# Two-layer hybrid trunk on one core: the next queries' projection issued ahead of the sliding keys' transposes, and the second layer's mixer norm at raised priority

## The chip, the core and the metric

The kernel runs on one core of one Trainium2 chip. The metric is the device time of one execution, in microseconds (us), as the median of repeated runs. In the code and in the profile the engines are PE (TensorE, the matmuls), DVE (VectorE), ACT (ScalarE), POOL (GpSimd) and SP (SyncE, which here issues the DMA transfers).

## What is computed

The reference is a trunk of two residual layers over 256 tokens of width 2048, all in float32. Layer 0 has the "even" mixer, layer 1 the "odd" one; behind each come a gated feed-forward part with a short convolution and a gated embedding. Cut to what matters here:

```python
for i in range(2):
    h = rms_norm(x, attn_norm[i])
    if i == 0:                                   # even mixer
        proj = h @ w_in_even[0]
        c_q, c_kv, k_idx, w_idx, qb, kb, vb = split(proj)
        # A: indexer scores pick the top 64 keys, then attention with
        #    q = rms_norm(rms_norm(c_q) @ w_uq) over the latents c_kv
        y_a = dsa_attention(c_q, c_kv, k_idx, w_idx, ...)
        # B: sliding-window attention, keys kb normed per head
        y_b = swa_sink_attention(qb, kb, vb, ...)
        y = concat(y_a, y_b) @ w_out_even[0]
    else:                                        # odd mixer
        y = forgetting_attention(h @ w_in_odd[0], ...) @ w_out_odd[0]
    x = x + y
    x = x + conv_ffn(rms_norm(x, ffn_norm[i]), ...)
    gate = sigmoid(rms_norm(x, ple_norm[i]) @ w_ple_gate[i])
    x = x + gate * (p[i] @ w_ple_proj[i])
```

## The kernel before

**Products.** The 256 tokens are two blocks `b` of 128 rows; the residual `x` stays on the chip in four column chunks `xs[b][j]` of 512. Every large product is made of matmuls of 128 by 128 by 512. `load` (L104) brings a piece of a weight of 1 MB into `raw`, which has three buffers; `granule` splits each half of it into a rounded high part `whi` on ACT (L116) and the rest `wlo` on DVE (L117), five buffers each. `Acc.add` (L144) then issues three matmuls for each pair of tiles (high by high, high by low, low by high) into two PSUM banks `ps_mm`, one for each block; three banks go round under that tag. A piece of 1 MB feeds 24 matmuls, and its `raw` buffer is free for the next load when DVE has made the second `wlo`.

**Norm.** `norm` (L177 to L195) makes the transposed, split left operand of a projection. For each chunk `j` and block `b` it multiplies `xs[b][j]` by a gain that SP loads (L177, two buffers), on DVE into a tile `xg` (L190), transposes that on PE in four pieces (L171, PSUM tag `ps_ax`, two banks), and splits the result with ACT (L123) and DVE (L124) into tiles called `n` (mixer norms) or `np` (gate norm). The row scale `rstd` is put on later, behind the product.

**Even mixer.** `proj_a(c)` makes the queries of four A heads: two products with `w_uq` (`cc`), each copied out of PSUM by ACT into an `xg` tile (L469), squared (L472) and transposed on PE (L211) into `qaT`, which DVE copies (L216); then comes a reciprocal square root, a chain of small DVE steps (L75 to L84). After `proj_a(0)` the indexer's scores and the top-64 search (L503, L504) run on DVE. Then the keys and values of the B heads are projected; each block's keys go into a tile `kk` of tag `xg` (L524), are squared and summed (`ssq_heads`), scaled by the reciprocal square root of the sums (`heads_rstd`, L328 to L331; L531) and transposed into `kbT` (L211, L214). `proj_a(1)` follows, then the values `vA` of the A heads (L547), the first A attention `att_a(0)` and the B queries (`proj_b`).

**Buffers and order.** The pool `work` has tags `xg`, `y` and `junk` with two buffers each. A framework orders the instructions: each engine's row is fixed before the run by a scheduler that takes instructions in the order of the code, unless a block stands in `tc.high_priority(offset=PR)`, with PR = 300, which lets its instructions go ahead of work that stands before it in the code. The gate norm in `ple_gate` (`np`) stands in such a block; the odd mixer's norm (`n1`) does not. An engine works through its row in order, so an instruction that waits holds all that stands behind it. SP's row holds all loads.

Of the kernel before, what the change touches and what calls it, by code (L numbers as in the profile page):

```python
# [9 lines left out]
F32 = mybir.dt.float32  # L10
# [6 lines left out]
P = 128  # L17
# [21 lines left out]
PR = 300  # L39
# [9 lines left out]
def trunk(ctx, tc, t, onehot, out):  # L49
# [7 lines left out]
    work = ctx.enter_context(tc.tile_pool(name="work", bufs=2))  # L57
# [12 lines left out]
    def rsqrt(dst, src, n, scale, post=1.0):  # L70

        v, y, a = (sm.tile([P, NT, 8], F32, tag="rq_" + c, name="rq_" + c)[:, :, :n] for c in "vya")
        if len(src.shape) == 2:
            v, y, a = v[:, :, 0], y[:, :, 0], a[:, :, 0]
        nc.vector.tensor_scalar(v, src, scale, EPS, op0=ALU.mult, op1=ALU.add)  # L75
        nc.vector.tensor_scalar(a.bitcast(I32), v.bitcast(I32), 1, None, op0=ALU.logical_shift_right)
        nc.vector.tensor_scalar(y.bitcast(I32), a.bitcast(I32), -1.0, MAGIC, op0=ALU.mult, op1=ALU.add)
        for it in range(3):
            nc.vector.scalar_tensor_tensor(a, y, -0.5, v, op0=ALU.mult, op1=ALU.mult)
            nc.vector.tensor_tensor(a, a, y, op=ALU.mult)  # L80
            last = it == 2
            nc.vector.scalar_tensor_tensor(dst if last and post == 1.0 else y, a, 1.5, y, op0=ALU.add, op1=ALU.mult)
        if post != 1.0:
            nc.vector.tensor_scalar(dst, y, post, None, op0=ALU.mult)  # L84
# [64 lines left out]
    def moving(src, c0, ncols, lhs, nktiles, nk=4):  # L149
        a = Acc(ncols, nktiles)  # L150
        a.add(src, c0, lhs, list(range(nktiles)), nk)
        return a.ps
# [5 lines left out]
    def make_ht(name):  # L158

        h = HT()  # L160
        h.t = [gp.tile([P, 4, 2, S], F32R, tag=f"ht{j}", name=f"{name}{j}") for j in range(4)]
        h.lhs = lambda k, b: tuple(h.t[k // 4][:, k % 4, m, b * P:(b + 1) * P] for m in range(2))
        h.rhs = lambda k: tuple(h.t[k // 4][:, k % 4, m, :] for m in range(2))
        h.both = lambda k: h.t[k // 4][:, k % 4].rearrange("p m s -> p (m s)")
        return h

    def transpose_split(h, j, b, src, tag="ax"):

        pt = psum(tag)
        for i in range(4):  # L170
            nc.tensor.transpose(pt[:, i * P:(i + 1) * P], src[:, i * P:(i + 1) * P], ident)  # L171
        split_evict(h.t[j][:, :, 0, b * P:(b + 1) * P], h.t[j][:, :, 1, b * P:(b + 1) * P],
                    pt.rearrange("p (a c) -> p a c", a=4))

    def load_gain(gain, j):
        g = gp.tile([P, 512], F32, tag="gbc", name="gain", bufs=2)
        nc.sync.dma_start(g, bcast_rows(gain[j * 512:(j + 1) * 512], 512))  # L177
        return g

    def norm(gain, name, loaded=()):  # L180

        h = make_ht(name)
        rstd = sm.tile([P, NT], F32, tag="rstd", name="rstd")
        h.rstd = [rstd[:, b:b + 1] for b in range(NT)]
        accs = sm.tile([P, NT, 4], F32, tag="ssx", name="ssx")
        for j in range(4):
            g = loaded[j] if j < len(loaded) else load_gain(gain, j)
            for b in range(NT):
                xg = work.tile([P, 512], F32, tag="xg", name="xg")
                nc.vector.tensor_tensor(xg, xs[b][j], g, op=ALU.mult)  # L190
                transpose_split(h, j, b, xg)
                junk = work.tile([P, 512], F32, tag="junk", name="junk")
                nc.scalar.activation(junk, xs[b][j], AF.Square, accum_out=accs[:, b, j:j + 1])
        tot = sm.tile([P, NT], F32, tag="sst", name="sst")
        nc.vector.tensor_reduce(tot, accs, axis=AX.X, op=ALU.add)  # L195
        rsqrt(rstd, tot, 1, 1.0 / D)
        return h
# [9 lines left out]
    def transpose_to(dst, src, n, parts=P, scale=None, eng="v"):  # L207

        pt = psum()
        for i in range(n):  # L210
            nc.tensor.transpose(pt[:, i * parts:(i + 1) * parts], src[:, i * P:(i + 1) * P], ident[:parts, :parts])  # L211
        v = pt[:, :n * parts].rearrange("p (a c) -> p a c", a=n)
        if scale is not None:
            nc.scalar.activation(dst, v, AF.Copy, scale=scale)  # L214
        elif eng == "v":
            nc.vector.tensor_copy(dst, v)  # L216
        else:
            nc.scalar.copy(dst, v)
# [97 lines left out]
    def ssq_heads(pool, ps, nh, dst):  # L316

        sq = work.tile([P, 512], F32, tag="junk", name="junk")
        nc.scalar.activation(sq[:, :nh * HD], ps, AF.Square)
        nc.vector.tensor_reduce(dst, sq[:, :nh * HD].rearrange("p (h d) -> p h d", h=nh), axis=AX.X, op=ALU.add)  # L320

    def heads_rstd(ssq, n, rx, width, post=1.0):


        r = sm.tile([P, NT, 8], F32, tag="hr", name="hr", bufs=HR)[:, :, :n]
        tmp = sm.tile([P, NT, 8], F32, tag="hrt", name="hrt")[:, :, :n]
        for b in range(NT):
            nc.vector.tensor_scalar(tmp[:, b], ssq[:, b], rx[b], rx[b], op0=ALU.mult, op1=ALU.mult)  # L328
        rsqrt(r, tmp, n, 1.0 / width)
        for b in range(NT):  # L330
            nc.vector.tensor_scalar(r[:, b], r[:, b], rx[b], post, op0=ALU.mult, op1=ALU.mult)  # L331
        return r


    def even_mixer(i, e):
        W = t["w_in_even"][e]
        with ExitStack() as es:
# [22 lines left out]
            h = norm(t["attn_norm"][i], "n0", gains)  # L360
# [98 lines left out]
            def proj_a(c):  # L459
                qT = []  # L460
                rqs = sm.tile([P, NT, 4], F32, tag="rqa", name="rqa", bufs=4)
                sqs = sm.tile([P, NT, 4], F32, tag="sqa", name="sqa")
                for cc in range(2):
                    ps = moving(t["a_w_uq"][e], (c * 2 + cc) * 512, 512, cq_lhs, 4)
                    qTc = ev.tile([P, 4, S], F32, tag="qT", name="qaT", bufs=6)
                    qT.append(qTc)
                    for b in range(NT):
                        qr = work.tile([P, 512], F32, tag="xg", name="xg")
                        nc.scalar.copy(qr, ps[b])  # L469
                        for z in range(2):  # L470
                            junk = work.tile([P, 512], F32, tag="junk", name="junk")
                            nc.scalar.activation(junk[:, :256], qr[:, z * 256:(z + 1) * 256], AF.Square,  # L472
                                                 accum_out=sqs[:, b, cc * 2 + z:cc * 2 + z + 1])
                        transpose_to(qTc[:, :, b * P:(b + 1) * P], qr, 4)
                rsqrt(rqs, sqs, 4, 1.0 / KV_LORA, post=KV_LORA ** -0.5)
                h_qa[c] = qT, rqs
# [42 lines left out]
            sk = sm.tile([P, NT, 2], F32, tag="sk", name="sk")  # L519
            kks = []  # L520
            for b in range(NT):
                kk = work.tile([P, 512], F32, tag="xg", name="xg")
                kks.append(kk)
                nc.scalar.copy(kk[:, 2 * P:3 * P], ps[b][:, :P])  # L524
                nc.scalar.activation(vB[:, b, :], ps[b][:, P:], AF.Copy, scale=rx[b])
                ssq_heads(ev, kk[:, 2 * P:3 * P], 2, sk[:, b])
            rk = heads_rstd(sk, 2, rx, HD)
            for b in range(NT):
                kk = kks[b]
# [3 lines left out]
                                            rk[:, b, g:g + 1], None, op0=ALU.mult)  # L533
                transpose_to(kbT[:, :, b * P:(b + 1) * P], kk, 2, scale=bg[:, 0:1])

            proj_a(1)

            vA = ev.tile([P, NT, H_A * HD], F32, name="vA")
            for c in range(2):
# [95 lines left out]
    def odd_mixer(i, o):  # L635
        W = t["w_in_odd"][o]
        HDC = H_C * HD
        with ExitStack() as es:
            od = es.enter_context(tc.tile_pool(name="od", bufs=1))
            h = norm(t["attn_norm"][i], "n1")  # L640
            rx = h.rstd
            cg = od.tile([P, 16], F32, name="cg")[:, :2]
            for m, nm in enumerate(("c_q_norm", "c_k_norm")):
# [253 lines left out]
    for i in range(2):  # L897
        if i % 2 == 0:
            even_mixer(i, i // 2)
        else:  # L900
            odd_mixer(i, i // 2)
        pd = ffn(i)
        ple_gate(i, pd, i == 1)
# [49 lines left out]
```

## Time and profile before

| | before |
|---|---|
| median of 3 runs | 2434.97 us (2433.53 to 2435.89) |
| the profiled execution | 2434.55 us |
| its span in the trace | 2432.8 us (1.75 us lie outside) |
| mean granted TensorE clock | 0.997 |
| PE busy | 2409.0 us, 99% |
| DVE busy | 1666.3 us, 68% |
| ACT busy | 1253.0 us, 52% |
| DMA, queue of the loads | 57.8% of 16 engines |

Times in the trace are us from the start of the span. The granted clock is a share of full speed: 1.00 is 2.4 GHz and 0.50 is 1.2 GHz; a mean between them says that a stretch held both. In a row of the timeline, what stands in brackets is the idle time of the engine before that row and the instruction that ended it.

### The profile page before, as it was taken

The page shows a single profiled execution, that of the slowest core. Times are in us where ns is not written, and L with a number is a line of the kernel's source. Part 1 is how long each engine was busy: PE and PEld are TensorE (multiplying, and loading weights), DVE is VectorE, ACT ScalarE, POOL GpSimd, SP SyncE. Part 2 cuts the span into 40 slices and gives each one's busy share as a digit, 9 for nine tenths or more (in the row PEclk, how much of TensorE's full clock was granted, in tenths as well). Part 3 has the DMA queues.
Part 4 walks back from the last instruction along what each step waited for, and adds up shares of the span by engine and source line. Part 5 has one row for each costly group of instructions (what it writes and reads, how often), then busy time and mean ns, then how long its engine had stood idle before and what let it go on. Part 6 is the DMA issues. An engine that isn't in the chain of part 4 may idle for free.

```text
span 2432.8 us, 32646 instructions
## 1 busy us (share of the span) xinstructions
PE 2409.0 (99%) x12530; PEld 2022.7 (83%) x12530; DVE 1666.3 (68%) x2670; ACT 1253.0 (52%) x1977; POOL 62.5 (3%) x138
## 2 busy tenths in 40 slices
PE   8999999999999999999999999999999999999999
PEld 6778788888888888888778777888888888888887
DVE  7777976777546777556676777677776457776564
ACT  6556655555335555444555555465554345555443
POOL 0000100000000000000030110000000000000000
PEclk9999999999999999999999999999999999999999
DMA  8444457666556665656565555576665566665564
GB/s 275 134 140 151 138 174 229 189 190 191 186 187 198 191 187 183 200 187 220 163 213 167 182 182 171 165 232 192 191 190 179 188 195 190 186 191 193 190 200 160
DMA packets 334001, 454.27 MB, mean 187 GB/s; under 512 B 15807, under 2 KB 210019, under 8 KB 333844
## 3 DMA queue, kind: packets, MB, share of 16 engines
q1 hardware_dynamic: 332468, 447.89, 57.8%
q0 software_dynamic: 1376, 4.28, 0.5%
q8 instruction: 99, 1.62, 0.3%
q14 instruction: 58, 0.48, 0.1%
HBM read 445.76 MB, written 6.37 MB: 186 GB/s over the span
## 4 chain that ended last, share of the span: by engine, by line
PE 88%; issue 7%; DMA 2%; DVE 2%; ACT 0%; POOL 0%; SPq 0%; DVEq 0%; ACTq 0%; POOLq 0%
PE ps_mm L144 43%; PE ps_mm L839 13%; PE ps_qk L839 13%; PE ps_mm L843 7%; PE ps_qk L843 7%; PE ps_qk L255 2%; DMA raw<-in_w_in_even_dram 1%; PE ps_o L294 1%; PE ps_ax L280 1%; DMA pled<-y 1%; PE ps_ax L211 1%; DVE wlo L117 1%; PE ps_ax L171 1%; PE ps_ax L454 0%; PE ps_qk L492 0%
## 5 line engine op out<-in xcount | busy, mean ns | idle before, releaser
L117 DVE TENSOR_TENSOR wlo<-raw,whi 128x1024 fp32r<-128x1024 f32 (+1 forms) x846 | 980.7, 1169 | 598.1 <-ACT whi L116 399.2
L116 ACT CAST whi<-raw 128x1024 fp32r<-128x1024 f32 (+1 forms) x846 | 835.5, 1005 | 947.3 <-PE ps_mm L144 507.8
L839 PE MATMUL ps_mm<-nf,whi 128*128 128x512 f32 x1376 | 345.0, 392 | 0.6 <-ACT y L799 0.6
L839 PE MATMUL ps_qk<-nf,whi 128*128 128x512 f32 x1376 | 341.7, 390 | 0.5 <-ACT whi L116 0.5
L144 PE MATMUL ps_mm<-whi,n 128*128 128x512 f32 (+2 forms) x1088 | 336.5, 388 | 2.3 <-ACT n L123 1.9
L839 PEld LDWEIGHTS ps_qk<-nf,whi 128*128 128x128 f32 x1376 | 257.5, 188 | 54.0 <-ACT whi L116 1.1
L839 PEld LDWEIGHTS ps_mm<-nf,whi 128*128 128x128 f32 x1376 | 247.6, 189 | 45.6 <-ACT y L799 1.2
L144 PE MATMUL ps_mm<-whi,glo 128*128 128x512 f32 x688 | 271.4, 395 | 0.0
L144 PE MATMUL ps_mm<-wlo,ghi 128*128 128x512 f32 x688 | 271.1, 395 | 0.0
L144 PE MATMUL ps_mm<-whi,ghi 128*128 128x512 f32 x688 | 270.6, 395 | 0.0
L144 PEld LDWEIGHTS ps_mm<-whi,n 128*128 128x128 f32 x1088 | 202.2, 190 | 46.2 <-issue 6.7
L144 PE MATMUL ps_mm<-wlo,n 128*128 128x512 f32 (+2 forms) x544 | 210.7, 388 | 0.3 <-DVE wlo L117 0.3
L843 PEld LDWEIGHTS ps_mm<-nf,wlo 128*128 128x128 f32 x1376 | 187.7, 190 | 13.4
L843 PE MATMUL ps_qk<-nf,wlo 128*128 128x256 f32 x1376 | 193.4, 283 | 0.0
L843 PE MATMUL ps_mm<-nf,wlo 128*128 128x256 f32 x1376 | 191.9, 282 | 0.0
L843 PEld LDWEIGHTS ps_qk<-nf,wlo 128*128 128x128 f32 x1376 | 178.2, 192 | 0.8
L144 PE MATMUL ps_mm<-whi,np 128*128 128x512 f32 x512 | 158.8, 390 | 0.0
L144 PEld LDWEIGHTS ps_mm<-whi,glo 128*128 128x128 f32 x688 | 129.6, 188 | 30.2
L144 PEld LDWEIGHTS ps_mm<-wlo,ghi 128*128 128x128 f32 x688 | 129.6, 188 | 30.0
L144 PEld LDWEIGHTS ps_mm<-whi,ghi 128*128 128x128 f32 x688 | 129.5, 188 | 29.5
L144 PEld LDWEIGHTS ps_mm<-wlo,n 128*128 128x128 f32 x544 | 103.2, 190 | 20.6 <-issue 1.4
L144 PEld LDWEIGHTS ps_mm<-whi,np 128*128 128x128 f32 x512 | 96.0, 188 | 19.7
(215 smaller groups left out, 2473.2 us busy)
## 6 DMA issues: line engine op xcount, KB each, us to landing
raw<-in_w_up_dram SPq DMA_DIRECT2D x168, 1024.0 KB, 5.3
raw<-in_w_down_dram SPq DMA_DIRECT2D x80, 1024.0 KB, 5.1
raw<-in_w_in_odd_dram SPq DMA_DIRECT2D x48, 1024.0 KB, 5.1
raw<-in_w_ple_gate_dram SPq DMA_DIRECT2D x32, 1024.0 KB, 5.2
raw<-in_w_out_even_dram SPq DMA_DIRECT2D x16, 1024.0 KB, 5.1
raw<-in_w_out_odd_dram SPq DMA_DIRECT2D x16, 1024.0 KB, 5.1
raw<-in_a_w_uq_dram SPq DMA_DIRECT2D x8, 1024.0 KB, 5.4
raw<-in_w_in_even_dram SPq DMA_DIRECT2D x8, 1024.0 KB, 5.3
```

The costliest lines, as they stand in the source:

```text
L116: nc.scalar.copy(hi, v[:, z:z + m])
L117: nc.vector.tensor_tensor(lo, v[:, z:z + m], hi.bitcast(F32), op=ALU.subtract)
L144: nc.tensor.matmul(self.ps[b], l, r[i], start=self.n[b] == 0, stop=self.n[b] == 3 * self.total - 1)
L171: nc.tensor.transpose(pt[:, i * P:(i + 1) * P], src[:, i * P:(i + 1) * P], ident)
L211: nc.tensor.transpose(pt[:, i * parts:(i + 1) * parts], src[:, i * P:(i + 1) * P], ident[:parts, :parts])
L255: nc.tensor.matmul(pss[g][:, i * n:(i + 1) * n], lt, rh, start=c == 0, stop=c == len(pairs) - 1)
L280: nc.tensor.transpose(pt[:, (i * nk + kb) * P:(i * nk + kb + 1) * P], s[:, i, kb * P:(kb + 1) * P], ident)
L294: nc.tensor.matmul(o[z:z + HD, m // 2 * P:(m // 2 + 1) * P], vv(heads[mm], kb), pTs[g][:, (i * nk + kb) * P:(i * nk + kb + 1) * P], start= ...
L839: nc.tensor.matmul(pu[z], hi[k][:, cols[z]], h.both(k0 + k), start=k0 + k == 0, stop=k0 + k == KD - 1, skip_group_check=True)
L843: nc.tensor.matmul(pu[z][:, :S], lo[k][:, cols[z]], h.rhs(k0 + k)[0], start=False, stop=k0 + k == KD - 1, skip_group_check=True)
```

## The change

Two things are changed. In the even mixer the two key tiles `kk` of the B heads take the tag `y` in place of `xg`, and the call of `proj_a(1)` moves from behind the keys' transposes to the place between their squared sums and their reciprocal square root. In the odd mixer the norm stands in a block of raised priority, like that of `ple_gate`.

```diff
             for b in range(NT):
-                kk = work.tile([P, 512], F32, tag="xg", name="xg")
+                kk = work.tile([P, 512], F32, tag="y", name="kk")
                 kks.append(kk)
                 nc.scalar.copy(kk[:, 2 * P:3 * P], ps[b][:, :P])
                 nc.scalar.activation(vB[:, b, :], ps[b][:, P:], AF.Copy, scale=rx[b])
                 ssq_heads(ev, kk[:, 2 * P:3 * P], 2, sk[:, b])
+            proj_a(1)
+
+
             rk = heads_rstd(sk, 2, rx, HD)
...
                 transpose_to(kbT[:, :, b * P:(b + 1) * P], kk, 2, scale=bg[:, 0:1])
 
-            proj_a(1)
...
-            h = norm(t["attn_norm"][i], "n1")
+            with tc.high_priority(offset=PR):
+                h = norm(t["attn_norm"][i], "n1")
```

Each engine has as many instructions as before; their order differs in one stretch for each of the two edits, and is the same everywhere else.

**First place: PE at the keys' transposes.** Before, these rows stand at the end of the second product of `proj_a(1)`, block 0 (`ps_mm_1324`); `xg_1216` and `xg_1222` are the key tiles, `xg_1300` the first copied queries:

```order
L144 MATMUL ps_mm_1324<-wlo_1333,cq_hi_219 128x512
L144 MATMUL ps_mm_1324<-whi_1332,cq_lo_220 128x512
L211 MATMUL ps_ax_1251<-ident_75,xg_1216 128x128 x2
L211 MATMUL ps_ax_1257<-ident_75,xg_1222 128x128 x2
L211 MATMUL ps_ax_1306<-ident_75,xg_1300 128x128 x4
L144 MATMUL ps_mm_1325<-whi_1328,cq_hi_219 128x512
```

Now the queries' transposes stand at that point of PE's row, and the product runs on behind them (`ps_mm_1291` is the same product, renumbered):

```order
L144 MATMUL ps_mm_1291<-whi_1299,cq_hi_219 128x512
L211 MATMUL ps_ax_1273<-ident_75,xg_1267 128x128 x4
L144 MATMUL ps_mm_1291<-wlo_1300,cq_hi_219 128x512
L144 MATMUL ps_mm_1291<-whi_1299,cq_lo_220 128x512
L144 MATMUL ps_mm_1292<-whi_1295,cq_hi_219 128x512
```

The keys' transposes come later, in the middle of the first product of `proj_b`:

```order
L144 MATMUL ps_mm_1529<-wlo_1606,n02_102 128x512
L144 MATMUL ps_mm_1529<-whi_1605,n02_102 128x512
L211 MATMUL ps_ax_1391<-ident_75,kk_1216 128x128 x2
L211 MATMUL ps_ax_1397<-ident_75,kk_1222 128x128 x2
L144 MATMUL ps_mm_1530<-whi_1601,n02_102 128x512
```

Between the queries' first transposes and the keys', PE's row now holds 74 matmuls and 16 transposes, the queries' own.

**Second place: DVE at the keys' scaling.** Before, the key chain ends, the keys are scaled, and only then come the queries' copies:

```order
L82 SCALAR_TENSOR_TENSOR hr_1228<-rq_a_1234,rq_y_1233 128x2x2
L331 TENSOR_SCALAR hr_1228<-hr_1228,rstd_104 128x2 x2
L531 TENSOR_SCALAR xg_1216<-xg_1216,hr_1228 128x128 x2
L531 TENSOR_SCALAR xg_1222<-xg_1222,hr_1228 128x128 x2
L216 COPY qaT_1299<-ps_ax_1306 128x4x128
L117 TENSOR_TENSOR wlo_1572<-raw_1565,whi_1571 128x1024
```

Now the queries' copies go between the last steps of the top-64 search, and both square-root chains (`rq_..54` and `..52` of the queries, `rq_..74` and `..72` of the keys) start only behind them:

```order
L216 COPY qaT_1266<-ps_ax_1285 128x4x128
L504 MATCH_REPLACE score1_989<-m8_1050,score1_989 128x256
L117 TENSOR_TENSOR wlo_1572<-raw_1565,whi_1571 128x1024
L505 TENSOR_SCALAR score1_989<-score1_989 128x256
L506 TENSOR_SCALAR score1_989<-score1_989 128x256
L117 TENSOR_TENSOR wlo_1602<-raw_1599,whi_1601 128x1024
L216 COPY qaT_1327<-ps_ax_1334 128x4x128
L75 TENSOR_SCALAR rq_v_1352<-sqa_1229 128x2x4
L75 TENSOR_SCALAR rq_v_1372<-hrt_1369 128x2x2
```

The keys' scaling moved from the place ahead of the first copy to one behind all four.

**Third place: PE and SP at the odd mixer's norm.** Before, PE's row has the first eight transposes of the norm right behind the gate's last matmul (`ps_mm_10288`) and right ahead of the first matmuls that read their result (`n10`):

```order
L144 MATMUL ps_mm_10288<-wlo_10398,np3_9721 128x512
L144 MATMUL ps_mm_10288<-whi_10397,np3_9721 128x512
L171 MATMUL ps_ax_10450<-ident_75,xg_10448 128x128 x4
L171 MATMUL ps_ax_10461<-ident_75,xg_10459 128x128 x4
L144 MATMUL ps_mm_10573<-whi_10577,n10_10440 128x512
L144 MATMUL ps_mm_10573<-wlo_10578,n10_10440 128x512
```

Now the same eight stand one by one between matmuls of the gate's second column chunk; 16 more follow in groups of eight within the gate's last chunk, and the last eight in the odd projection:

```order
L144 MATMUL ps_mm_9988<-whi_10059,np2_9720 128x512
L171 MATMUL ps_ax_10450<-ident_75,xg_10448 128x128
L144 MATMUL ps_mm_9988<-wlo_10060,np2_9720 128x512
L171 MATMUL ps_ax_10450<-ident_75,xg_10448 128x128
L144 MATMUL ps_mm_9988<-whi_10059,np2_9720 128x512
```

In SP's row the last gain of this norm stood behind the odd projection's loads:

```order
L104 DMA raw_10643<-in_w_in_odd_dram 128x4x512
L104 DMA raw_10677<-in_w_in_odd_dram 128x4x512
L104 DMA raw_10758<-in_w_in_odd_dram 128x16x32
L177 DMA gain_10518<-in_attn_norm_dram 128x512
L177 DMA gain_14272<-in_ffn_norm_dram 128x512
```

It now stands ahead of the gate's last three loads:

```order
L890 DMA pp_10281<-pled_3486 128x512
L177 DMA gain_10518<-in_attn_norm_dram 128x512
L104 DMA raw_10323<-in_w_ple_gate_dram 128x4x512
L104 DMA raw_10357<-in_w_ple_gate_dram 128x4x512
L104 DMA raw_10391<-in_w_ple_gate_dram 128x4x512
```

The load of the gain moved ahead of seven loads of 1 MB and one small one, and it waits, as every load does, until its buffer is free. Two gains of the feed-forward norm moved up likewise, each past two weight loads or fewer.

## Rows read from the trace of the kernel before

**Rows 1.** The page: busy time, share of the span, instructions of each engine.
```profile
PE 2409.0 (99%) x12530; PEld 2022.7 (83%) x12530; DVE 1666.3 (68%) x2670; ACT 1253.0 (52%) x1977; POOL 62.5 (3%) x138
```
**Rows 2.** PE's waits: line, waited for what: us in total, times, longest.
```profile
PE ps_ax L211 <- DVE xg L531: 3.7, 1, 3.7
PE ps_mm L144 <- ACT n L123: 1.9, 1, 1.9
...
PE ps_ax L171 <- DVE n L124: 1.2, 1, 1.2
...
PE ps_ax L211 <- ACT xg L469: 0.6, 1, 0.6
```
**Rows 3.** Windows: us, busy by engine, granted clock (fourth column from the right: PEclk).
```profile
40.00:60.00 20.00, 17.90 (x104) 15.16 (x103) 18.73 (x52) 12.92 (x23) 1.15 (x2) 1.00 0.94 294
...
120.00:125.00 5.00, 4.38 (x14) 3.52 (x15) 1.13 (x4) 4.33 (x16) 0.00 (x0) 0.50 0.01 2
...
155.00:170.00 15.00, 15.00 (x84) 12.07 (x84) 15.00 (x35) 11.43 (x30) 0.00 (x0) 1.00 0.47 145
...
1180.00:1185.00 5.00, 3.76 (x12) 2.90 (x11) 3.49 (x9) 4.54 (x15) 0.00 (x0) 0.58 0.17 53
```
**Rows 4.** Timeline of PE at the keys: start, us, line, out<-in, [idle before <-releaser].
```profile
115.55 0.39 PE L144 MATMUL ps_mm<-wlo,cq_hi 128*128 128x512 f32 x1
115.78 0.39 PE L144 MATMUL ps_mm<-whi,cq_lo 128*128 128x512 f32 x1
119.91 1.12 PE L211 MATMUL ps_ax<-ident,xg 128*128 128x128 f32 x4 [3.74 <-DVE xg L531]
...
126.25 0.39 PE L144 MATMUL ps_mm<-whi,cq_hi 128*128 128x512 f32 x1
```
**Rows 5.** Timeline of DVE, 113 to 123 us.
```profile
113.21 1.23 DVE L117 TENSOR_TENSOR wlo<-raw,whi 128x1024 fp32r<-128x1024 f32 x1
...
117.39 0.43 DVE L503 MAX8 m<-score 128x8 f32<-128x256 f32 x1
...
118.26 0.15 DVE L82 SCALAR_TENSOR_TENSOR rq_y<-rq_a,rq_y 128x4 f32<-128x4 f32 x1
...
119.57 0.87 DVE L531 TENSOR_SCALAR xg<-xg,hr 128x128 f32<-128x128 f32 x4
122.80 0.69 DVE L216 COPY qaT<-ps_ax 128x512 f32<-128x512 f32 x1 [2.35 <-PE ps_ax L211]
```
**Rows 6.** The chain that ended last: start, us, a run of matmuls, count.
```profile
1097.39 78.92 PE ps_mm L144 x348
```
**Rows 7.** Timeline of PE at the end of the gate, layer 0.
```profile
1176.15 1.03 PE L171 MATMUL ps_ax<-ident,xg 128*128 128x128 f32 x8
1179.12 0.50 PE L144 MATMUL ps_mm<-whi,n 128*128 128x512 f32 x1 [1.93 <-ACT n L123]
...
1181.59 1.09 PE L171 MATMUL ps_ax<-ident,xg 128*128 128x128 f32 x4 [1.24 <-DVE n L124]
...
1187.44 0.79 PE L144 MATMUL ps_mm<-whi,n 128*128 128x512 f32 x2
```
**Rows 8.** Timeline of DVE and then ACT, same place.
```profile
1177.21 0.68 DVE L190 TENSOR_TENSOR xg<-x,gain 128x512 f32<-128x512 f32 x1
...
1178.48 1.07 ACT L123 CAST n<-ps_ax 128x512 fp32r<-128x512 f32 x2
```
**Rows 9.** Timeline of PE where the gate norm's transposes stand among matmuls.
```profile
1029.09 0.40 PE L144 MATMUL ps_mm<-whi,ghi 128*128 128x512 f32 x1
1029.32 0.27 PE L171 MATMUL ps_ax<-ident,xg 128*128 128x128 f32 x1
...
1031.13 0.40 PE L144 MATMUL ps_mm<-wlo,ghi 128*128 128x512 f32 x1
...
1095.42 0.60 PE L171 MATMUL ps_ax<-ident,xg 128*128 128x128 f32 x4
1095.77 0.71 PE L144 MATMUL ps_mm<-whi,np 128*128 128x512 f32 x2
```
**Rows 10.** Timeline of PE, a wait early in the program.
```profile
59.39 0.73 PE L144 MATMUL ps_mm<-whi,cq_hi 128*128 128x512 f32 x2 [1.14 <-ACT whi L116]
```
**Rows 11.** The page, DMA issues: count, KB each, us from issue to landing.
```profile
raw<-in_w_in_odd_dram SPq DMA_DIRECT2D x48, 1024.0 KB, 5.1
```

## The prediction, made before the changed kernel was run

> **What bounds the kernel now.** I read the page's busy line first, then PE's list of waits, then the granted clock by stretch, then the timelines at the two places that the list names. PE is busy for 2409.0 of 2432.8 us [rows 1], so only what PE does not do in the other 23.8 us, or does at a low clock, can be won. The list of waits says where it stood still: 3.7 us once for the scaled keys (L531), with 0.6 us for the copied queries (L469) right behind, and 1.9 and 1.2 us for the odd mixer's first normed tiles (L123, L124) [rows 2]. That is 7.4 us of standing, all at the two places that the diff touches.
>
> A wait of PE here costs more than itself. In the 5 us behind the first stop the granted clock is 0.50, which is 1.2 GHz, and behind the second it is 0.58 on average [rows 3]; the mean of the whole run is 0.997. So each place is priced by the time that its stretch takes over what its work takes at full clock. The prices: a matmul costs 78.92 / 348 = 0.227 us [rows 6], four transposes in a row 95.77 - 95.42 = 0.35 us, so 0.088 us each [rows 9].
>
> **Place A, the keys.** The stretch from the last matmul ahead of the stop (115.78) to the first one back at full clock (126.25) takes 10.47 us [rows 4]. It holds 10 matmuls (2.27 us) and 8 transposes (0.70 us), 2.97 us in all. Lost: 10.47 - 2.97 = **7.5 us**; 4.35 us of it are the two waits, 3.15 us the low clock.
>
> Why it stops: the two `xg` buffers are held by the key tiles until their transposes, and these wait for a chain of small DVE steps that stands among top-64 steps and `wlo` splits. The copies of the next queries need the same buffers, and the PSUM banks cannot be emptied without them. With the keys in `y`, the queries' copies no longer wait for the keys; with the call moved, PE's row has the queries' transposes where the keys' stood. The tag alone would leave the keys' transposes at that point, the move alone would leave the buffers held, so the two work together.
>
> Is the keys' scaling in time at its new place? PE gets there after the 74 matmuls and 16 transposes that now stand between: 74 x 0.227 + 16 x 0.088 = 18.2 us, counted from 115.55, the start of the matmul at whose place the queries' first transposes now stand [rows 4]: 133.8 us. DVE, counted from the `wlo` at 113.21 that stands in both orders [rows 5], has ahead of the end of the scaling: 6 `wlo` at 1.23 (7.4), 3 pairs of search steps at 118.26 - 117.39 = 0.87 (2.6), 2 threshold steps at no more than 0.43 each (0.9), 4 copies at 0.69 (2.8), 25 steps of the two chains at 0.15 (3.8), and the scaling with its two small steps at 0.87 + 0.3 (1.2), together 18.7 us: done at 131.9. That is 1.9 us to spare, with whole durations where instructions in a row overlap a little; but a chain step that waits for the one ahead of it can take longer than 0.15, and with 0.20 each the margin is 0.6 us. If it fails, PE waits for the difference alone. I take nothing for it; the bounds are 0 and 1 us.
>
> The queries' own transposes, at 115.55, stand 22 matmuls (5.0 us) behind the last matmul of the product whose copy they need; a copy of this size takes 0.69 us on DVE [rows 5], and ACT's cannot be far from it: no wait. The instructions between this place and about 180 us are the same on every engine, in another order, and the order of the attention's transposes is such that they come where DVE has them ready at about the old time; what PE draws forward is projection matmuls. So the 7.5 us should stay won. Bounds: 5.5 to 7.5.
>
> **Place B, the odd norm.** From the eight transposes at 1176.15 to the first matmul at full clock (1187.44) the trace has 11.29 us [rows 7], with 14 matmuls (3.18) and 16 transposes (1.40), 4.58 us of work. Lost: **6.7 us**, of which 3.17 are waits and 3.5 the clock.
>
> Why: the norm's products on DVE came only at 1177.21 and the split of the transposes at 1178.48 [rows 8], all between the last gate matmul and the first that reads `n10`. With raised priority 24 of the 32 transposes run inside the gate's product, up to some 50 us earlier, and the last eight in the first product of the projection. Chunk 0 of `x` is final when the gate's first column chunk is done, chunks 1 and 2 each one product (48 x 2 matmuls, 21.8 us) later, so only chunk 3 can press: it is first read as the fourth part of the projection, 72 matmuls or 16 us behind its start, while its chain (gate, product, transpose, split) took 3 us for the first chunk here. That cover is ample.
>
> What it adds: nothing in count, but single transposes between matmuls. The trace has the same pattern at the gate's own norm, which stands in such a block: from 1029.09 to 1031.13 PE took 2.04 us for 5 matmuls and 8 transposes [rows 9], which by the prices above are 1.84. So **0.2 us** is paid back, and PE has no wait there. SP's row has the last gain ahead of seven loads; it waits for a product on DVE that is done well before the load behind it may start, since that needs the next `wlo` in DVE's row. I take 0, and the other end is a rival below.
>
> **Sum.** 7.5 + 6.7 - 0.2 = 14.0 us off the profiled 2434.55, which is 0.42 below the median: 2420.5 for the profile, 2421.0 for the median of runs.
>
> **Rivals.**
>
> *The first softmax gives A back.* PE would reach `att_a(0)` up to 7.5 us earlier, and DVE is busy for 15.00 of 15 us from 155 to 170 [rows 3]. If a transpose of the softmax came ahead of its tile, PE would wait there. Against it: the first attention's transposes moved behind more matmuls. Given back in full it leaves B: 2434.97 - 6.5 = 2428.5; in part, 2423 to 2428. Chance 0.08.
>
> *Short waits drop the clock.* If a short wait remains at A (the keys come late by up to 1 us), the clock could fall for it as it did behind the long one: 3.15 us and the wait, so about 2425. Against it: a wait of 1.14 us at 59.39 [rows 10] lies in a stretch with a granted clock of 1.00 [rows 3]. The Trainium skill, "TensorE: Matmul & The Clock Gate", section "A second HAM failure mode: psum-queue depth-cycling", says that a PE that idles briefly and often between groups of matmuls, as PSUM banks go round, has its clock pulled down again and again. By that rule any short wait left here is dear; the trace disagrees for a single one of 1.14 us. Chance 0.04.
>
> *It does nothing.* The waits return at the new places, since the product that frees the buffer or the norm's first chunk is late for a reason that the list of waits hides: 2433.5 to 2436. Against it: two waits of different causes would both have to return. Chance 0.05.
>
> *The gains hold up SP: slower.* Three gain loads now stand ahead of weight loads in SP's row. A gain whose buffer comes free late stops every load behind it. PE eats 1 MB in 24 x 0.227 = 5.4 us, a load takes 5.1 us to land [rows 11], so a hold longer than the three `raw` buffers cover (about 11 us) stops PE for a load, 5.1 us, and the clock's 3.5 come on top: 8.6 us each. One such would leave 2434.97 - 7.5 + 8.6 = 2436; two, from which it is clearly slower, 2444.7. Against it: the norm's products come early in DVE's row. Chance 0.03.
>
> **How the numbers follow.** The forecast, both gaps closed, has 0.80 and gives 2419.5 to 2422.5. Runs of one kernel spread by 1.2 us to a side, and small waits elsewhere could shrink: low end 2418.5. The first two rivals reach from 2423 to 2428.5; most of them, by weight, lies below 2426.5, which is the high end. About 0.2% or 4.9 us is what a measurement can tell from no change: faster means below 2430.1. Forecast, first and second rival are faster (0.92), the third is the same (0.05), the last slower (0.03).
>
> **What would show it.** Right: the L531 wait (now at its moved line) and the L123 and L124 waits are gone from PE's list; the granted clock is 1.00 at 120 and at 1175 us; PE's idle time falls from 23.8 to about 16.5; the gate's last matmul stands some 5 us earlier in the trace (7.5 less the 24 transposes, 2.1 us, that the gate then holds), and the last instruction 14. Wrong in A: a new wait for DVE at the keys' transposes near 134, or in the softmax between 145 and 172. Wrong in B: a wait on a fourth-chunk tile in the odd projection, or a stretch without DMA ahead of it. Anything past 2428 says that one of the two places was not won.

## The result: 12.4 us faster, both stops gone

| | before | changed |
|---|---|---|
| median of 5 runs each | 2434.97 us (2432.89 to 2440.76) | 2422.56 us (2421.22 to 2424.51) |
| the profiled execution | 2434.55 us | 2421.22 us |
| its span in the trace | 2432.8 us | 2419.4 us |

The ratio of the runs is 0.9946, with a 95% interval from 0.9932 to 0.9961. 2421.0 us was predicted, with a range from 2418.5 to 2426.5.

Busy time of the changed kernel, and the longest of PE's waits (line, waited for what: us in total, times, longest), which answer [rows 1, 2]:

```profile
PE 2403.6 (99%) x12530; PEld 2019.4 (83%) x12530; DVE 1664.0 (69%) x2670; ACT 1252.6 (52%) x1977; POOL 63.4 (3%) x138
...
PE ps_ax L171 <- DVE xg L190: 5.9, 1, 5.9
PE ps_mm L144 <- ACT whi L116: 1.7, 3, 1.1
PE ps_ax L204 <- DVE nf L124: 0.8, 2, 0.5
PE ps_mm L144 <- DVE wlo L117: 0.8, 2, 0.5
PE ps_mm L842 <- ACT y L802: 0.6, 1, 0.6
```

None of the four waits of [rows 2] is left, and no new one has come. What stands here was there before too. PE's idle time is 2419.4 - 2403.6 = 15.8 us, where it was 23.8 and some 16.5 were expected; the gate's last matmul starts at 1171.85 in place of 1175.92, so 4.1 us earlier where some 5 were expected. The windows at both places, to hold against [rows 3] (the granted clock is the third column from the right, there as here):

```profile
115.00:120.00 5.00, 5.00 (x27) 4.16 (x26) 4.76 (x12) 3.38 (x12) 0.00 (x0) 1.00 0.66 210
120.00:125.00 5.00, 5.00 (x27) 4.14 (x26) 4.45 (x18) 2.74 (x7) 0.00 (x0) 1.00 0.60 181
...
1170.00:1175.00 5.00, 5.00 (x23) 4.13 (x23) 4.97 (x8) 4.28 (x7) 0.00 (x0) 1.00 0.42 131
1175.00:1180.00 5.00, 5.00 (x25) 4.15 (x24) 3.16 (x5) 4.94 (x13) 0.00 (x0) 1.00 0.36 87
```

PE is busy for 5.00 of 5 us in each, at a granted clock of 1.00. At place A the keys are ready well ahead of PE. First DVE's scaling, then PE's first transpose of the keys, from the timelines of the changed kernel:

```profile
129.51 0.87 DVE L534 TENSOR_SCALAR kk<-kk,hr 128x128 f32<-128x128 f32 x4
...
134.39 0.60 PE L211 MATMUL ps_ax<-ident,kk 128*128 128x128 f32 x4
```

DVE is done at 130.38, PE comes at 134.39: 4.0 us to spare, where the prediction had 1.9.

**Two stretches as a measure.** The times of single runs spread by several us, so the places are compared by stretches of the trace, each between two instructions that stand in every kernel here. Stretch A runs from the first matmul of `proj_a(1)` to a product of the second A attention (L294); stretch B from the first transpose of the gate's norm [rows 9] to the forget gate's first matmul (L726; L729 in the changed kernel). The rows of before are the first three, those of the changed kernel the last four:

```profile
107.82 0.40 PE L144 MATMUL ps_mm<-whi,cq_hi 128*128 128x512 f32 x1
...
203.77 0.44 PE L294 MATMUL ps_o<-att_p,vA 128*64 128x128 f32 x4
...
1215.93 0.40 PE L726 MATMUL ps_ax<-n,whi 128*32 128x256 f32 x2
```

```profile
107.94 0.40 PE L144 MATMUL ps_mm<-whi,cq_hi 128*128 128x512 f32 x1
...
196.78 0.44 PE L294 MATMUL ps_o<-att_p,vA 128*64 128x128 f32 x4
...
1022.47 0.27 PE L171 MATMUL ps_ax<-ident,xg 128*128 128x128 f32 x1
...
1202.58 0.40 PE L729 MATMUL ps_ax<-n,whi 128*32 128x256 f32 x2
```

A takes 203.77 - 107.82 = 95.95 us before and 88.84 changed: **7.1 us**. B takes 1215.93 - 1029.32 = 186.61 and 180.11: **6.5 us**. Together 13.6; the spans differ by 13.4. The same two stretches in the other kernels' profiles, in us:

| kernel | stretch A | stretch B |
|---|---|---|
| before, two profiles | 95.95, 95.88 | 186.61, 185.14 |
| changed, two profiles | 88.84, 88.85 | 180.11, 180.11 |
| keys changed alone, two profiles | 88.84, 88.84 | 183.82, 185.31 |
| tag alone | 89.52 | 185.35 |
| norm raised alone | 96.18 | 180.11 |
| first chunk of the norm alone | 95.86 | 180.17 |
| tag and norm, no move | 89.52 | 180.11 |
| before, one square-root step | 93.66 | 186.44 |
| before, six square-root steps | 98.09 | 185.36 |
| changed, with a later load | 88.85 | 180.11 |

Where PE does not stop, the stretch of one order of instructions repeats to 0.01 us. Where it stops, the two places differ: the four profiles with the unchanged stop at A lie within 0.3 us (95.86 to 96.18), while at B the same two waits give stretches that differ by up to 2.8 us (183.82 to 186.61).

### The profile page after: what moved, and what is told of

Its sections match the earlier page's. It is cut to its first block, busy times and chain, and to the rows that moved or that the text cites. A ratio compares the mean times of both kernels' runs of the same rounds, so it can differ in the third digit from the quotient of the medians.

```text
span 2419.4 us, 32642 instructions
## 1 busy us (share of the span) xinstructions
PE 2403.6 (99%) x12530; PEld 2019.4 (83%) x12530; DVE 1664.0 (69%) x2670; ACT 1252.6 (52%) x1977; POOL 63.4 (3%) x138
## 4 chain that ended last, share of the span: by engine, by line
PE 88%; issue 7%; DMA 3%; DVE 1%; ACT 0%; POOL 0%; SPq 0%; DVEq 0%; ACTq 0%; POOLq 0%
PE ps_mm L144 43%; PE ps_mm L842 13%; PE ps_qk L842 13%; PE ps_mm L846 7%; PE ps_qk L846 7%; PE ps_qk L255 2%; PE ps_o L294 1%; PE ps_ax L280 1%; PE ps_ax L211 1%; PE ps_ax L171 1%; DMA pled<-y 1%; DMA gain<-in_attn_norm_dram 1%; PE ps_ax L454 0%; DMA raw<-in_w_in_even_dram 0%; PE ps_qk L492 0%
## 5 line engine op out<-in xcount | busy, mean ns | idle before, releaser
L842 PE MATMUL ps_mm<-nf,whi 128*128 128x512 f32 x1376 | 345.1, 393 | 0.7 <-ACT y L802 0.6
L842 PE MATMUL ps_qk<-nf,whi 128*128 128x512 f32 x1376 | 341.6, 390 | 0.4 <-ACT whi L116 0.4
L842 PEld LDWEIGHTS ps_qk<-nf,whi 128*128 128x128 f32 x1376 | 257.6, 188 | 53.7 <-ACT whi L116 0.9
L842 PEld LDWEIGHTS ps_mm<-nf,whi 128*128 128x128 f32 x1376 | 247.8, 189 | 45.5 <-ACT y L802 1.3
```

Of the source, the lines that this page charges most:

```text
L842: nc.tensor.matmul(pu[z], hi[k][:, cols[z]], h.both(k0 + k), start=k0 + k == 0, stop=k0 + k == KD - 1, skip_group_check=True)
```

## The experiments

**Each edit alone.** The norm raised alone is the last hunk of the diff, the keys changed alone the others.

> Only the odd mixer's norm is raised; the even mixer is that of before. Theory (two separate places, whose gains add up): the kernel before minus the 6.5 us of place B, 2428.5 us, and PE's stop of 3.7 us for the scaled keys stays as it was, with the low clock behind it. Rival (the places are linked, the second only took up slack that the first had left): less than 4 us, above 2431.

> Only the even mixer is changed (tag and place of the call). Theory: the changed kernel's trace stands 7.0 us ahead of before from 204 us on (203.77 against 196.78 for the same matmul of the attention), so about 2428.0 us, and PE's waits for L123 and L124 (1.9 and 1.2 us) and the low clock behind them stay. Rival (the gain of A is partly given back before the end): above 2430.

Measured: norm alone 2430.57 us, ratio 0.9982 (0.9973 to 0.9991) of before at 2435.78; keys alone 2429.18 us, 0.9971 (0.9960 to 0.9981). The ratios say 4.4 and 7.1 us, together 11.5; those of the changed kernel, 0.9946 here and 0.9953 in a second set of runs, say 13.1 and 11.4. The 7.0 us expected of the keys came. Of the 6.5 us expected of the norm 4.4 came, with an interval from 2.2 to 6.6, so the runs alone do not rule out the rival of less than 4 us. The stretches do: the two places are separate, since stretch A of the norm alone is that of before to 0.3 us, its stretch B is that of the changed kernel, and the keys alone have the changed kernel's stretch A and a stop in stretch B. What did not come as expected is the first profile of the keys alone. The odd norm's stop is there, the low clock is not. PE's timeline at the stop, and the window behind it:

```profile
1169.16 1.03 PE L171 MATMUL ps_ax<-ident,xg 128*128 128x128 f32 x8
1172.13 0.50 PE L144 MATMUL ps_mm<-whi,n 128*128 128x512 f32 x1 [1.93 <-ACT n L123]
...
1174.60 0.63 PE L171 MATMUL ps_ax<-ident,xg 128*128 128x128 f32 x4 [1.25 <-DVE n L124]
1174.98 0.71 PE L144 MATMUL ps_mm<-whi,n 128*128 128x512 f32 x2
...
1175.76 0.62 PE L144 MATMUL ps_mm<-whi,n 128*128 128x512 f32 x2
...
1177.38 0.60 PE L171 MATMUL ps_ax<-ident,xg 128*128 128x128 f32 x4
...
1175.00:1180.00 5.00, 5.00 (x27) 4.13 (x25) 3.22 (x15) 4.25 (x11) 0.00 (x0) 1.00 0.00 0
```

The waits are those of [rows 7] to 0.01 us, but the matmuls behind them run at full speed. From the eight transposes to the second group of four behind them, at 1177.38, it takes 8.22 us here; in the first profile of before the same work, up to the group at 1186.74, took 1186.74 - 1176.15 = 10.59. So 2.4 us of what the prediction read off place B belonged to that one execution.

**The same kernels, profiled once more.**

> The kernel before, unchanged, profiled once more. If the low clock is bound to the stops: 0.50 at 120 to 125 us and 0.58 at 1180 to 1185 us, as in the first profile. If it comes by the execution: the same waits (3.7, 0.6, 1.9, 1.2 us) with another clock behind at least one of them, and a span that differs by 1.5 to 3 us at that place.

> The keys changed alone, profiled once more. The waits at the odd norm are 1.9 and 1.2 us again. If the clock behind them comes by the execution: a mean of 0.5 to 1.0 in the 5 us behind the second wait, not bound to repeat the 1.00 of the first profile of this kernel; from the eight transposes to the third group of four behind them 8.2 us where it stays full, up to 10.6 where it falls.

Before again (2435.55 us): the same four waits. At place A nothing changed, the clock is 0.77 for 115 to 130 us in both profiles. At place B it is 0.75 and 0.91 at 1180 to 1185 and 1185 to 1190, against 0.58 and 0.74, and stretch B is 1.5 us shorter than in the first profile. Keys alone again (2428.75 us): the two waits are 1.93 and 1.26, the clock falls this time, and the same piece takes 1180.11 - 1170.37 = 9.74 us. Its timeline, beside the one above:

```profile
1170.37 1.03 PE L171 MATMUL ps_ax<-ident,xg 128*128 128x128 f32 x8
1173.34 0.50 PE L144 MATMUL ps_mm<-whi,n 128*128 128x512 f32 x1 [1.93 <-ACT n L123]
...
1175.80 1.09 PE L171 MATMUL ps_ax<-ident,xg 128*128 128x128 f32 x4 [1.26 <-DVE n L124]
1176.54 1.20 PE L144 MATMUL ps_mm<-whi,n 128*128 128x512 f32 x2
1177.97 1.05 PE L144 MATMUL ps_mm<-whi,n 128*128 128x512 f32 x2
...
1180.11 0.60 PE L171 MATMUL ps_ax<-ident,xg 128*128 128x128 f32 x4
```

Two rows of two matmuls are listed with 1.20 and 1.05 us where the first profile has 0.71 and 0.62. Of seven profiles with this stop (before and the keys alone twice each, the tag alone, one and six square-root steps), six show the low clock behind it, for stretches of different length, and one does not. Mean of the seven stretches B: 185.4 us, so 5.3 us above the kernels without the stop.

**Does place A need tag and move both?**

```diff
-                kk = work.tile([P, 512], F32, tag="xg", name="xg")
+                kk = work.tile([P, 512], F32, tag="y", name="kk")
```

> The key tiles take the tag y, the call of proj_a(1) stays behind the keys' transposes. Theory of the prediction (the tag alone leaves the keys' transposes where PE stops): the 3.7 us wait and the low clock stay, the 0.6 us wait for the copied queries goes, about 2434. Rival (the held buffers are the whole cause): the order built for this kernel has the keys' transposes some 35 rows later on PE, behind matmuls of proj_b; then the long wait is gone, and what stays are short waits, some 1 us in all, at the queries' transposes: 2435 - 7.0 + 1 = 2429, and if these short waits pull the clock down too, about 2432.

> The tag y for the key tiles and the raised norm, without the moved call. Theory (from the trace of the tag alone, where PE stops for some 1.2 us in all at 127 to 129 us with the clock at full): 1 to 1.5 us above the changed kernel, 2423.5 to 2424 where that has 2422.5. Rival of the prediction (tag and move are both needed): without the move the 3.7 us wait returns, 2428 or more.

> The changed kernel once more, beside the others of this call. All theories: 2421 to 2424.5 us; no wait of PE above 1.2 us behind the first 60 us.

Measured: tag alone 2428.15 us, ratio 0.9976 (0.9965 to 0.9986). Tag and norm 2423.30, ratio 0.9953 (0.9940 to 0.9965), beside the changed kernel's 2423.12, 0.9953 (0.9939 to 0.9966). The two kernels are 0.2 us apart, where 1 to 1.5 were expected. The prediction's sentence that the tag alone would leave the stop falls. One expectation for the changed kernel was missed: its second profile has a wait above 1.2 us behind the first 60, one of 1.43 us at 1609.80 in the second layer's feed-forward part (L842 for ACT's L802). The first profile has none there, before has one of 0.31 us, and the first chunk of the norm alone one of 2.06: this place too differs between executions, far from both edits. PE's timeline in the kernel with the tag alone, and one window:

```profile
127.12 0.60 PE L211 MATMUL ps_ax<-ident,kk 128*128 128x128 f32 x4
128.06 1.09 PE L211 MATMUL ps_ax<-ident,xg 128*128 128x128 f32 x8 [0.35 <-ACT kbT L214]
129.39 0.50 PE L144 MATMUL ps_mm<-whi,n 128*128 128x512 f32 x1 [0.24 <-ACT xg L469]
...
125.00:130.00 5.00, 4.41 (x26) 3.40 (x25) 1.25 (x2) 2.09 (x5) 0.00 (x0) 1.00 0.20 78
```

With the buffers free, the scheduler itself puts the keys' transposes behind matmuls of `proj_b`; two waits of 0.35 and 0.24 us are left, at full clock. Stretch A is 89.52 us: the tag gives 6.4 of the 7.1 us, the move 0.7 more, which the runs can't tell apart. The move without the tag was not run; by the code, the queries' copies would then wait for buffers that the keys give back only behind them.

**How much of the norm has to be raised?** Only chunk 0's gain, products, transposes and split go into the block of raised priority:

```diff
-            g = loaded[j] if j < len(loaded) else load_gain(gain, j)
-            for b in range(NT):
+            with (tc.high_priority(offset=PR) if j in up else ExitStack()):
+                g = loaded[j] if j < len(loaded) else load_gain(gain, j)
+                for b in range(NT):
...
-            h = norm(t["attn_norm"][i], "n1")
+            h = norm(t["attn_norm"][i], "n1", up=(0,))
```

> Only chunk 0 of the odd mixer's norm (its gain, its two products, eight transposes and their split) is raised, chunks 1 to 3 stand as before; even mixer as before. Theory A (all of the loss came from the first chunk's chain, the later chunks are covered by matmuls of the projection): as norm_alone, 2428.5 us. Theory B (the second wait, 1.2 us for L124, is a chain of its own that comes with each chunk): one wait of 1 to 2 us stays, and the low clock with it, 2431 to 2433.

Measured: 2430.67 us, ratio 0.9980 (0.9971 to 0.9989), against 2430.57 for the whole norm. Neither of the two waits is in PE's list, so theory A holds: chunk 0 is what PE waited for, and the wait for L124 went with it. That this second wait was for the PSUM banks, which the split of the same chunk still held, fits its row (a transpose into `ps_ax` that waits for the split), but was not tried by itself.

**What does a stop cost?** The keys' reciprocal square root gets one step, or six, in place of three, which shortens or lengthens the chain that PE waits for; everything else stays as before.

```diff
-            rk = heads_rstd(sk, 2, rx, HD)
+            rk = heads_rstd(sk, 2, rx, HD, its=1)
```

> The kernel before, with one step in place of three in the reciprocal square root of the sliding keys (two steps of three left out): six small DVE steps fewer in the chain that PE waits for. The wait for L531 falls from 3.7 to about 2.2 us, the one for L469 stays at 0.6 to 0.9. Theory A (the low clock comes with the length of the stop): at this length the granted clock behind it stays at 1.00, as behind the two waits of the norm in the trace of the keys changed alone, and the place loses some 4 us where before lost 7.5. Theory B (the low clock comes or not by the execution, whatever the length above 1 us): it can fall to 0.5 to 0.7 here too, and then the place loses 5.5 to 6 us.

> The kernel before with six steps in place of three in the reciprocal square root of the sliding keys: nine more small DVE steps in the chain. The wait for L531 grows from 3.7 to about 5.5 us. Theory (each stop costs its length and, if the clock falls, some 1 to 3 us that do not grow with it): the stretch from the last matmul ahead of the stop to the ninth behind it takes 12 us where before took 10.2. Rival (the price of the clock grows with the stop): 13.5 us or more.

PE's timeline, one step first, then six:

```profile
115.90 0.39 PE L144 MATMUL ps_mm<-whi,cq_lo 128*128 128x512 f32 x1
118.31 0.91 PE L211 MATMUL ps_ax<-ident,xg 128*128 128x128 f32 x4 [2.02 <-DVE xg L531]
...
121.43 0.63 PE L144 MATMUL ps_mm<-whi,cq_lo 128*128 128x512 f32 x1
121.85 0.63 PE L144 MATMUL ps_mm<-whi,cq_hi 128*128 128x512 f32 x1
...
123.80 0.40 PE L144 MATMUL ps_mm<-whi,cq_lo 128*128 128x512 f32 x1
```

```profile
115.82 0.39 PE L144 MATMUL ps_mm<-whi,cq_lo 128*128 128x512 f32 x1
121.72 1.11 PE L211 MATMUL ps_ax<-ident,xg 128*128 128x128 f32 x4 [5.52 <-DVE xg L531]
...
127.78 0.63 PE L144 MATMUL ps_mm<-whi,cq_lo 128*128 128x512 f32 x1
```

With one step the wait is 2.02 us, 1.72 less, and stretch A is 2.3 us shorter; the matmuls behind still start 0.42 us apart (121.43 to 121.85), the pace of 1.2 GHz. So theory A, that a stop of this length leaves the clock at 1.00, falls. Theory B is right that the clock can fall here, but not in its price: from 115.90 to 123.80 it takes 7.9 us for 9 matmuls and 8 transposes, 2.7 us of work, so the place loses 5.2 us by the prediction's way of counting and not 5.5 to 6. With six the wait is 5.52 us, 1.78 more, and stretch A is 2.1 us longer; to the ninth matmul behind the stop it takes 127.78 - 115.82 = 11.96 us, the 12 of the theory, not 13.5. Over the changed kernel's stretch A, less the two waits at the place, there remain 4.8 - 2.7 = 2.1 us with one step, 7.1 - 4.4 = 2.7 with three and 9.3 - 6.1 = 3.2 with six: at this place a stop costs its length, and then 2 to 3 us, which grow by 1.1 us while the waits grow by 3.4. The windows from 115 to 130 us, with one step, three and six:

```profile
115.00:130.00 15.00, 12.32 (x54) 9.61 (x53) 10.55 (x34) 8.20 (x25) 0.00 (x0) 0.89 0.42 130
```

```profile
115.00:130.00 15.00, 10.64 (x44) 8.31 (x43) 9.45 (x30) 8.18 (x24) 0.00 (x0) 0.77 0.29 83
```

```profile
115.00:130.00 15.00, 8.87 (x33) 6.76 (x32) 9.07 (x37) 6.44 (x19) 0.00 (x0) 0.66 0.22 70
```

The longer the stop, the lower the clock over the stretch; the three other profiles with the unchanged stop have 0.77 too. In none of the six does the clock stay at 1.00 here, so that part of theory B (it comes or not by the execution) is shown at place B alone. Both runs, 2432.88 and 2435.32 us, are single ones.

**A version meant to take an early wait away.** The second half of `w_uv` is loaded later:

```diff
                 wuv = ev.tile([P, 1024], F32, tag="toe", name="wuv", bufs=2)
+                if c:
+                    nc.gpsimd.tensor_copy(wuv[:, 511:513], qiT[1][:, 0, :2])
```

> The changed kernel, and the two loads of the second half of w_uv (L545, c = 1) wait for a two-element copy on POOL from the indexer queries, so they come some 10 us later than at 54 us, behind the weight load that PE waits for at 59.6. In ten profiles so far PE stands there for 0.4, 0.5 and 1.1 us, and in four of the ten the granted clock fell behind it, at a price of 1.6 us. Theory (the small loads crowd out the 1 MB load): the 1.1 us wait goes, and with it the low clock: 1 us less in the trace up to 108 us, and 2421 to 2422.5 in the runs. Rival (the wait is that load's own time of landing): the wait stays within 0.3 us, and the time is that of the changed kernel, 2422.5 to 2423.

Measured: 2422.93 us, ratio 0.9951 (0.9937 to 0.9964), so nothing won over the changed kernel. The load comes at 80.2 us in place of 54.7, later than the 10 us expected. The theory falls and the rival stands: the wait of 1.1 us stays, with the small load out of its way. The order built for this kernel brings another wait to the same stretch, 1.79 us at the one-hot products (L400), and the clock falls behind it (0.63 for 55 to 60 us):

```profile
54.65 0.82 PE L400 MATMUL ps_ax<-oh 33*16 33x384 f32 x2 [1.79 <-DVE cq_lo L124]
...
PE ps_mm L144 <- ACT whi L116: 1.5, 2, 1.1
```

## Why the prediction was right, and where it was off

**Reading the bound: right.** PE's 7.4 us of waits at two places and the low clock behind them were what the change could win, and that is what went. The rest of PE's list is as before, to 0.2 us.

**Place A: mechanism right, size 0.4 us too high, one sentence wrong.** 7.5 us were forecast, the stretch shows 7.1. The term took transposes at 0.088 us each; when a group of four stands among matmuls, the second matmul behind it comes later, as the changed kernel's timeline shows:

```profile
115.68 0.60 PE L211 MATMUL ps_ax<-ident,xg 128*128 128x128 f32 x4
116.03 0.48 PE L144 MATMUL ps_mm<-wlo,cq_hi 128*128 128x512 f32 x1
116.34 0.40 PE L144 MATMUL ps_mm<-whi,cq_lo 128*128 128x512 f32 x1
116.58 0.40 PE L144 MATMUL ps_mm<-whi,cq_hi 128*128 128x512 f32 x1
```

From 116.03 to 116.34 it is 0.31 us, not 0.23. In the kernel before, the two groups stood at the stop, where this is part of the time counted as lost; now they pay 0.08 each, 0.16 in all. The other 0.2 us stay open. The margin at the keys' new place was underrated (4.0 for 1.9 us): DVE was done 1.5 us sooner than summed, since whole durations were added where its instructions overlap, and PE came 0.6 us later. The sentence that failed is the one on tag and move: it took the scheduler's order as fixed under the tag alone.

**Place B: mechanism right, the clock's share over-sized.** 6.7 us lost and 0.2 paid back were forecast, and the two first profiles differ by just that, 6.5. But the 3.5 us put down to the clock and its surroundings were one draw. The stop costs 183.82 - 180.11 = 3.7 us where the clock stays, 6.5 where it falls longest, and 5.3 in the mean of seven. The step that failed is to price the clock from one execution. The first profile of before, from which the forecast was read, has the longest stretch B of the seven: 1.2 us above their mean. With 7.1 for A and 5.3 for B the sum is 12.4 us, 1.6 below the forecast of 14.0. That it meets the difference of the medians to the tenth is luck: the second set of runs has 11.8, and the interval of the ratio reaches from 9.5 to 16.6 us.

**The rivals.** The first softmax gave nothing back: stretch A, which holds it, is 88.84 or 88.85 us in all five profiles with tag and move, and the two of the changed kernel and the two of the keys alone have no wait of PE in it. The gain loads did not hold up SP: no new wait in stretch B. "It does nothing" is out. The rival of the short waits was wrong where it was placed (the two short waits that the tag without the move leaves stay at full clock), yet the reading against it was too quick, as the last section shows.

## What to carry to other kernels

A stop of the matmul engine is priced by the stretch from the last instruction at full pace to the next one, not by the wait alone; but the clock's part of that price can differ between executions (a stop of the same waits cost from 0.5 to 3.3 us beyond them at place B, and the same within 0.3 us at place A), so read it from several profiles, or state it as a range from none to what you see. When a tile waits in a shared pool for work further down, giving it a tag whose buffers lie idle can free the scheduler to do the rest; moving the code as well gave little here. Raising the priority of the norm helped through its first chunk, the only one that the next product reads at once.

## What the runs showed of the hardware

**The clock behind a short wait is a matter of the execution.** The prediction held [rows 10] against the rival: a wait of 1.14 us in a stretch at full clock. In twelve profiles this place has the same instructions (the thirteenth is the kernel with the later load), and in five of them the clock falls there, to a mean of 0.66 over 55 to 60 us. The norm alone, PE's timeline and window:

```profile
54.19 0.73 PE L144 MATMUL ps_mm<-whi,cq_hi 128*128 128x512 f32 x2 [0.44 <-ACT whi L116]
...
55.45 0.50 PE L144 MATMUL ps_mm<-wlo,cq_hi 128*128 128x512 f32 x1 [0.52 <-DVE wlo L117]
...
56.42 0.63 PE L144 MATMUL ps_mm<-wlo,cq_hi 128*128 128x512 f32 x1
56.85 0.63 PE L144 MATMUL ps_mm<-whi,cq_lo 128*128 128x512 f32 x1
...
60.72 0.73 PE L144 MATMUL ps_mm<-whi,cq_hi 128*128 128x512 f32 x2 [1.13 <-ACT whi L116]
...
55.00:60.00 5.00, 4.14 (x10) 2.80 (x10) 3.94 (x19) 0.63 (x2) 0.93 (x2) 0.66 0.86 225
```

The same first wait in the profile of before:

```profile
54.43 0.73 PE L144 MATMUL ps_mm<-whi,cq_hi 128*128 128x512 f32 x2 [0.44 <-ACT whi L116]
```

The clock falls before the wait of 1.13 us, behind two of 0.44 and 0.52, not behind it as the expectation of the last experiment had it. From the first of them to the long one it is 60.72 - 54.19 = 6.53 us in the norm alone, and 59.39 - 54.43 = 4.96 in before [rows 10]: 1.6 us that come and go between executions of the same instructions. Over the twelve profiles it is 6.35 to 6.53 in the five where the clock falls, and 4.95 to 4.99 in the seven where it stays.

The Trainium skill, "TensorE: Matmul & The Clock Gate", section "Part 1: The HAM clock gate", says that the number of slow matmuls at the start of a kernel differs from run to run of that kernel. The traces show the like in the middle of one: behind one and the same stop the time spreads over 2.8 us (stretch B). Of the section "A second HAM failure mode: psum-queue depth-cycling" of the same page of the Trainium skill, which the prediction weighed, the runs bear out a part: the clock fell behind brief waits at this place in five of twelve profiles, and did not behind the two at 128 us in the profiles of the tag alone and of tag and norm. That section of the Trainium skill speaks of idling that comes often, so the prediction's reading of it, that any short wait is dear, went further than its words.
